# Mixer 0's recurrence: eight chunks formed at once, one product and one copy per chunk in the chain

## The chip, the cores and the metric

The kernel runs on 1 core of one Trainium2 chip. A core has five engines with their own instruction streams: TensorE (PE, matrix products into PSUM; its weight loads are shown as PEld), VectorE (DVE), ScalarE (ACT), GpSimd (POOL) and SyncE (SP, which issues DMAs). PSUM has eight banks; one bank holds 128 x 512 float32. The metric is the device time of one execution in microseconds (us); lower is better.

## The reference

A causal trunk of two layers over 1024 tokens of width 1024. All that the change touches is mixer A of layer 0, the RWKV-7 recurrence, 8 heads of 64:

```
xs = rms_norm(x) @ w_in ... shifted, split into r, k, v and low-rank w, a, g
decay w = exp(-exp(w_log));  kk = k*k_k / |k*k_k|;  k = k*(1 + (a-1)*k_a)
per head, per token t (S is 64 x 64, starts at 0):
    sa = S @ (-kk_t)
    S  = S * w_t + sa (x) (kk_t*a_t) + v_t (x) k_t
    y_t = S @ r_t
y: group norm per head, + bonus, * gate g; concatenated with mixer B (gated conv of width 3) @ w_out, added to h
```

After that mixer come a squared-ReLU MLP, a per-layer embedding, and layer 1 (a diagonal state-space mixer, its MLP and embedding) and a last RMSNorm. Those parts are as they were.

## The kernel before, in words

**Layout.** Activations are kept feature-major: 128 features on the partitions, 512 tokens (half the sequence) on the free axis. The sequence is done as two halves, A and B. A pair of heads fills 128 partitions, so a half has four pairs, and mixer 0 has eight (half, pair) units, numbered 0 to 7. Within a unit the 512 tokens are 8 chunks of 64.

**The large products.** Each float32 matrix product with a weight is three fp32r products (high and low halves of both operands, `mm3`, L157 to L159). One "unit" of filler work is one such triple: a tile `ps_z` of the input projection has 8 of them (`zmm`), a tile of the output projection (`ps_wo`, jobs named W) has one per input block. Weights come by DMA on SP's queue (`wload`, L142), are rounded by ACT (L145), and POOL forms the low half (L146).

**The recurrence of one (half, pair).** Four generators, each a list of steps divided by `yield`:

- `rwkv_f`: decay, its running product `L`, `eL`, the norm of kk (tiles `ps_w`, `ps_a`, `ps_ss`, `ps_rn`).
- `rwkv_a`: the scaled operands `RA` (r and -kk times the decay since the chunk's start) and `KB` (k and kk*a divided by it); the masked score matrices `SC` of every chunk (`ps_sc`); the bonus (`ps_bo`); then `inverse`: the inverse of a unit triangular 64 x 64 matrix per chunk and head, by doubling in 32 x 32 blocks (`ps_ix`, `ps_it`, `ps_fx`, `ps_ft`), each product followed by a VectorE operation that the next product needs. Its result is `Rf`.
- `rwkv_c`: first `V`, `K`, `B` with tokens on the partitions (`by_token`: four transposes and four ACT copies each, L687 and L691). Then for each chunk, in turn, with the state `S`: `ps_c` = scores x V + RA x S, an ACT copy to `rhs` (L725); `ps_sa` = Rf x rhs, an ACT copy to `SA` (L735); `ps_s` = K x V + B x SA, and VectorE makes the new state from it (`Sn`, L747) with the old state scaled by ACT (`SD`, L730); `ps_y` gives the output of the chunk, copied by VectorE to `Y` (L748). Three steps a chunk, 24 in all, each one waiting on a copy out of PSUM that the step before it made possible.
- `rwkv_g`: group norm of `Y`, transposes back (`ps_yt`, L779), gain and bias, the gate product (`ps_gt`, L788), and the split for the output projection (`yah`, `yal`).

**What sets the order.** TensorE's order is written by hand (`manual_schedule`); the other engines' orders are made by a scheduler at build time. `mixer0_run` goes through ten stages. In a stage up to four generators run side by side for different pairs (`crit`: for example c of pair 1, a of pair 2, g of pair 0, f of pair 3), one step of each at a time; after each step of theirs, units of the large products are put in (`MIX_JOBS` says which, `MIX_UNITS` how many in the stage; the stage has as many steps as its longest generator, `MIX_STEPS`). So TensorE's stream is: a burst of small products (one step of each generator), some units of three 512-column products as cover, the next burst, and so on. Jobs: z = the projections for r, k, v of a pair, C = the three projections of a conv group, W = a piece of the output projection, X = load and transpose x of half B, S = swap of the residual halves through DRAM, R = the sum of squares of half A's residual for the next norm (23 `yield`s, nearly none with a TensorE product), L = the low-rank projections.

**Norm of the input.** The 1/rms of a half (`rstd`) is formed inside the first `zmm` that ends: product `ps_ms`, square root on ACT, reciprocal on DVE, product `ps_rs` (L213 to L223), all at one place in TensorE's order.

**PSUM.** Three banks for the large products (`ps_z`, `ps_wo`, `ps_xt`), two with tag `a` (f and a), three with tag `b` (c and g).

Of the kernel before, what the change touches and what calls it, by code (L numbers as in the profile page):

```python
# [5 lines left out]
F32 = mybir.dt.float32  # L6
# [51 lines left out]
class Trunk:  # L58
# [16 lines left out]
    def setup2(self):  # L75
# [11 lines left out]
        mp = self.mp  # L87
        self.lwa = mp.tile([P, 512], F32, name="lwa")
# [400 lines left out]
    def zmm(self, st, col, out):  # L489
# [8 lines left out]
        if "rstd" not in st:  # L498
            st["rstd"] = list(self.rstd_steps(st["acc"], pool=self.pc, tag="a"))[1][0]
# [88 lines left out]
    def rwkv_f(self, st, p, cx):  # L588
# [38 lines left out]
        for _ in range(5):  # L627
            yield
# [6 lines left out]
    def rwkv_a(self, st, p, cx):  # L635
# [968 lines left out]
```

## Time and profile before

| | us |
|---|---|
| median of 3 runs | 2757.8 (2756.29 to 2758.71) |
| the profiled execution | 2759.97 |
| its span, first to last instruction | 2758.1 |
| end of mixer 0 (last `ps_wo` product) in that span | about 749 |
| TensorE busy over the span | 2608.0 |

A row of the timeline reads: start, duration, engine, line, operation, out<-in, count; the brackets give the idle time of the engine before it and what ended it. A float32 product of two operands that are not rounded shows two records per instruction, an fp32r product one. A product's duration is longer than the distance to the next one, since products overlap in the array; the price of a product in a stream is read from the starts. The view of stretches gives, for each stretch of time, the busy time of each engine with its count of instructions, the granted TensorE clock (PEclk, 1.00 is full speed) and the share of the DMA engines.

### The profile page before, as it was taken

Reading aid. Unit: us, or ns where it says so; the run is one execution under the profiler, and the core shown is the slowest. Engines: PE = TensorE matmul, PEld = TensorE weight load, DVE = VectorE, ACT = ScalarE, POOL = GpSimd, SP = SyncE. Lnnn points to the kernel's source line nnn. Section 1 sums busy time; section 2 is a strip of 40 time slices with the busy share of each in tenths; the row PEclk is TensorE's granted clock in tenths of the full one; section 3 lists DMA queues with packets and bytes.
Section 4 is the critical chain, followed back from the end, with each engine's and each line's share of the span. In section 5 each row is a group of like instructions: output and inputs, shape, how many; then the busy total and the mean of one; then the engine's idle time right before and its main releaser. Section 6 shows DMA issues by size and latency. Waiting matters only on the chain.

```text
span 2758.1 us, 47137 instructions
## 1 busy us (share of the span) xinstructions
PE 2608.0 (95%) x18029; PEld 2043.5 (74%) x18029; DVE 1933.9 (70%) x3103; ACT 1089.9 (40%) x2145; POOL 1195.4 (43%) x1771
## 2 busy tenths in 40 slices
PE   7999899999898899999999997999999999999998
PEld 5776676666576677777788776788788888888786
DVE  5565666665599899899778648622577777777854
ACT  4334444443432344454554535412433333333432
POOL 4443334532443577777764406411343443343410
PEclk9999999999999899999999999999999999999999
DMA  4222211411211233333121324311111111111121
GB/s 108 58 69 87 91 56 45 142 44 41 73 47 43 64 93 95 92 96 96 61 65 45 92 64 145 104 46 46 35 54 53 47 54 50 50 54 47 49 77 61
DMA packets 273437, 189.08 MB, mean 69 GB/s; under 512 B 36110, under 2 KB 255484, under 8 KB 273212
## 3 DMA queue, kind: packets, MB, share of 16 engines
q1 hardware_dynamic: 249232, 158.26, 19.4%
q10 hardware_dynamic: 21084, 19.17, 2.7%
q0 software_dynamic: 2896, 8.65, 0.9%
q8 instruction: 142, 2.33, 0.3%
q14 instruction: 83, 0.68, 0.1%
HBM read 156.92 MB, written 29.10 MB: 67 GB/s over the span
## 4 chain that ended last, share of the span: by engine, by line
PE 66%; DVE 15%; POOL 7%; issue 6%; ACT 3%; DMA 2%; SPq 0%; ACTq 0%; POOLq 0%; DVEq 0%
PE ps_dnx L352 9%; PE ps_up L159 6%; PE ps_up L157 6%; PE ps_up L158 6%; PE ps_dny L352 5%; PE ps_z L157 3%; PE ps_z L158 2%; PE ps_z L159 2%; PE ps_gl L157 2%; PE ps_gl L159 2%; PE ps_gl L158 2%; DVE ha L355 2%; PE ps_g L157 2%; PE ps_g L159 2%; PE ps_g L158 2%
## 5 line engine op out<-in xcount | busy, mean ns | idle before, releaser
L158 PE MATMUL ps_up<-prl,uwh 128*128 128x512 f32 x1024 | 403.9, 394 | 2.5 <-DVE prl L175 2.5
L159 PE MATMUL ps_up<-prh,uwl 128*128 128x512 f32 x1024 | 406.2, 397 | 0.0
L157 PE MATMUL ps_up<-prh,uwh 128*128 128x512 f32 x1024 | 405.2, 396 | 0.7 <-ACT prh L174 0.7
L258 POOL TENSOR_TENSOR uwl<-uraw,uwh 128x512 fp32r<-128x512 f32 x136 | 187.7, 1380 | 170.3 <-ACT uwh L255 169.4
L158 PEld LDWEIGHTS ps_up<-prl,uwh 128*128 128x128 f32 x1024 | 193.8, 189 | 49.3 <-DVE prl L175 4.1
L157 PEld LDWEIGHTS ps_up<-prh,uwh 128*128 128x128 f32 x1024 | 194.1, 190 | 46.4 <-ACT prh L174 1.2
L159 PEld LDWEIGHTS ps_up<-prh,uwl 128*128 128x128 f32 x1024 | 193.3, 189 | 44.6
L352 PE MATMUL ps_dnx<-hidh,whi 128*128 128x512 f32 x480 | 197.7, 412 | 29.7 <-DVE ha L355 29.6
L146 POOL TENSOR_TENSOR wlo<-wraw,whi 128x1024 fp32r<-128x1024 f32 x66 | 159.7, 2421 | 138.2 <-ACT whi L145 137.2
L271 POOL TENSOR_TENSOR draw<-draw 128x128 f32<-128x128 f32 x120 | 59.8, 499 | 339.2 <-DMA draw<-in_l_ffn_down_dram 274.9
L355 DVE TENSOR_TENSOR h<-h,ps_dnx 128x512 f32<-128x512 f32 x240 | 163.8, 683 | 57.8 <-PE ps_dnx L352 56.4
L196 POOL TENSOR_TENSOR acc<-acc,sq 128x512 f32<-128x512 f32 x70 | 105.6, 1517 | 220.4 <-ACT sq L195 219.6
L352 PE MATMUL ps_dnx<-hidl,whi 128*128 128x512 f32 x480 | 189.0, 394 | 3.7 <-DVE hidl L317 3.7
L352 PE MATMUL ps_dnx<-hidh,wlo 128*128 128x512 f32 x480 | 189.2, 394 | 2.4 <-DVE wlo L281 2.4
L157 PE MATMUL ps_z<-prh,whi 128*128 128x512 f32 x416 | 190.6, 458 | 0.0
L255 ACT CAST uwh<-uraw 128x512 fp32r<-128x512 f32 x136 | 84.2, 619 | 243.4 <-PE ps_up L158 227.7
L355 DVE TENSOR_TENSOR ha<-ha,ps_dnx 128x512 f32<-128x512 f32 x240 | 163.4, 681 | 18.4 <-PE ps_dnx L352 18.2
L145 ACT CAST whi<-wraw 128x1024 fp32r<-128x1024 f32 x104 | 108.8, 1047 | 166.5 <-PE ps_z L158 72.0
L159 PE MATMUL ps_z<-prh,wlo 128*128 128x512 f32 x416 | 168.1, 404 | 1.6 <-POOL wlo L146 1.6
L158 PE MATMUL ps_z<-prl,whi 128*128 128x512 f32 x416 | 167.7, 403 | 0.6 <-DVE prl L478 0.6
L317 DVE TENSOR_TENSOR hidl<-r_up,hidh 128x512 fp32r<-128x512 f32 x188 | 151.9, 820 | 21.2 <-ACT r_up L313 16.4
L312 ACT ACTIVATE hidh<-r_up 128x512 fp32r<-128x512 f32 x98 | 61.9, 632 | 232.9 <-DVE r_up L309 226.3
(429 smaller groups left out, 6623.7 us busy)
## 6 DMA issues: line engine op xcount, KB each, us to landing
uraw<-in_l_ffn_up_dram SPq DMA_DIRECT2D x128, 256.0 KB
draw<-in_l_ffn_down_dram SPq DMA_DIRECT2D x120, 256.0 KB
wraw<-in_l_w_in_dram SPq DMA_DIRECT2D x52, 512.0 KB
s5w<-s5w SPq DMA_DIRECT2D x32, 384.0 KB
wraw<-in_l_w_out_dram SPq DMA_DIRECT2D x16, 512.0 KB
wraw<-in_l_ple_gate_dram SPq DMA_DIRECT2D x16, 512.0 KB
wraw<-in_l_glu_w_dram SPq DMA_DIRECT2D x16, 512.0 KB
toep<-kt ACTq DMA_DIRECT2D x32, 240.0 KB
```

The source lines that it names most:

```text
L145: nc.scalar.copy(hi[:, :n], raw[:, :n])
L146: self.lo_engine().tensor_sub(lo[:, :n], raw[:, :n], hi[:, :n].bitcast(F32))
L157: nc.tensor.matmul(ps, wh, xh, start=start, stop=False)
L158: nc.tensor.matmul(ps, wh, xl, start=False, stop=False)
L159: nc.tensor.matmul(ps, wl, xh, start=False, stop=stop)
L196: (eng or nc.vector).tensor_add(acc, acc, sq)
L255: A.copy(uw[m][0], raws["u"])
L258: nc.gpsimd.tensor_sub(uw[m][1], raws["u"], uw[m][0].bitcast(F32))
L312: A.activation(st[n][0], r, AF.Square)
L317: return lambda: eng.tensor_sub(st[nm][1], t, st[nm][0].bitcast(F32))
L352: nc.tensor.matmul(ps, w[:, a], v, start=id(ps) not in begun, stop=n == 2, skip_group_check=True)
L355: V.tensor_add(hv, hv, ps)
```

## The change

The recurrence is rewritten so that nothing but one product and one copy per chunk depends on the chunk before:

- For all 8 chunks at once, one bank each: `X` = scores x V (`ps_x`), `W` = Rf x At (`ps_wc`, where `At` is the -kk part of RA by token, a fourth `by_token`), `U` = Rf x X (`ps_u`), `T` = I + W x B (`ps_t`), `Yr` = RA + W x scores (`ps_yr`). X, W and U are copied out by ACT, T and Yr by VectorE additions (T with the new constant `eye`).
- `pG` holds K x V + B x U of all chunks in one bank of its own; in the chain, `ps_g` of chunk c gets T x S added, and one ACT copy scaled by the chunk's decay is the next state. After the last chunk `ps_y` is made for all chunks (three products a chunk) and copied by ACT once.
- `rwkv_a` has its VectorE work and scores in fewer, fuller steps; `inverse` begins right after the first scores. `rwkv_g` has the gate product one step after the transposes back.
- `MIX_STEPS` falls from 26/28/7/6/13 to 14/14/5/6/8; the jobs and units of the stages are dealt out anew (`W67a` from the start of its stage into a mix with the norm of half B, `C1` to `C7` later or earlier by a place, `R` behind `W45b` in the next stage, `W67b` into the last stage).
- `rstd` of each half is formed by a generator `scale` with a step between its products, filled with units.
- PSUM: tag `b` has two banks in place of three; the third is `g`.

```diff
-MIX_STEPS = [26, 28, 7, 6, 13]
-MIX_UNITS = [19, 52, 78, 51, 73, 47, 57, 42, 44, 38, 5]
-MIX_JOBS = ['z1 C0', 'C1 z2 C2 W45a', 'z3 X3', 'W67a M L z4 W01a', 'C4 z5', 'z6 W23a C5', 'z7 S W45b R', 'C6 W01b', 'C7 W67b', 'W2b W3b', '']
+MIX_STEPS = [14, 14, 5, 6, 8]
+MIX_UNITS = [19, 48, 64, 72, 72, 48, 40, 48, 40, 40, 24]
+MIX_JOBS = ['z1 C0', 'z2 C1 W45a', 'z3 C2 X3', 'N M L z4 W01a', 'z5 C4', 'z6 W23a', 'z7 C5 S', 'W45b R C6', 'W01b C7', 'W67b W2b W3b', '']
...
+        self.eye = mp.tile([P, 64], F32, name="eye")
+        nc.vector.tensor_add(self.eye, self.ident[:, 0:64], self.ident[:, 64:128])
...
-        if "rstd" not in st:
-            st["rstd"] = list(self.rstd_steps(st["acc"], pool=self.pc, tag="a"))[1][0]
...
+        def scores(m):
             for g in range(2):
                 ps = self.pc.tile([P, H], F32, tag="a", name="ps_sc")
                 for q in range(4):
                     for h in range(2):
                         hs = slice(64 * h, 64 * h + 64)
-                        nc.tensor.matmul(ps[hs, q * P:(q + 1) * P], KB[hs, m, 4 * g + q], RA[hs, 4 * g + q], start=True, stop=True)
+                        nc.tensor.matmul(ps[hs, q * P:(q + 1) * P].rearrange("p (a t) -> p a t", a=2), KB[hs, m, 4 * g + q],
+                                         RA[hs, :, 4 * g + q], start=True, stop=True)
                 nc.vector.tensor_mul(SC[m][:, 4 * g:4 * g + 4], ps.rearrange("p (c t) -> p c t", c=4),
                                      self.msc.rearrange("p (o t) -> p o t", o=1).broadcast_to([P, 4, P]))
-                yield
+        scores(1)
+        nc.vector.tensor_mul(KB[:, 0], v8(k2), v8(enL))
+        rk = cx["bo"] = self.rp.tile([P, H], F32, tag="rk", name="rk", bufs=3)
+        nc.vector.scalar_tensor_tensor(rk, r, self.c("l0_r_k", p), k2, ALU.mult, ALU.mult)
+        yield
+        inv = self.inverse(SC[1], cx)
+        next(inv)
+        scores(0)
+        yield
         ps = self.pc.tile([P, H], F32, tag="a", name="ps_bo")
         nc.tensor.matmul(ps, self.bd, rk, start=True, stop=True)
         nc.vector.tensor_mul(rk, ps, v)
-        yield from self.inverse(SC[1], cx)
-        yield
-
-    def by_token(self, src, tag):
-
-        nc = self.nc
-        ps = self.pc.tile([P, H], F32, tag="b", name="ps_" + tag)
+        yield from inv
...
-        def mm(ps, a, b, start, stop):
+        c8 = lambda n, k=1: self.rp.tile([P, 8, 64], F32, tag=n, name=n, bufs=k)
+
+        def bank(name, tag="b"):
+            return self.pc.tile([P, H], F32, tag=tag, name=name).rearrange("p (c f) -> p c f", f=64)
+
+        def mm(ps, c, a, b, start=True, stop=True):
             for s in hs:
-                nc.tensor.matmul(ps[s, 0:64], a[s], b[s], start=start, stop=stop, skip_group_check=True)
...
+                nc.tensor.matmul(ps[s, c], a[s], b[s], start=start, stop=stop, skip_group_check=True)
+
+        def each(ps, a, b):
+            for c in range(8):
+                mm(ps, c, a[:, c], b[:, c])
+
+        V, At, K, B = c8("Vt"), c8("At"), c8("Kt"), SB[:, :, 64:128]
+        flat = lambda t: t.rearrange("p c t -> p (c t)")
+        kb = cx["KB"]
+        self.by_token(flat(kb[:, 0]), K, "Kt")
+        self.by_token(flat(kb[:, 1]), B, "Bt")
+        yield
+        self.by_token(v, V, "Vt")
+        yield
+        self.by_token(flat(RA[:, 1]), At, "At")
+        yield
+        X = SK[:, :, 64:128]
+        px = bank("ps_x")
+        each(px, X, V)
+        nc.scalar.copy(X, px)
+        yield
+        pw = bank("ps_wc")
+        each(pw, Rf, At)
+        W = At
+        nc.scalar.copy(W, pw)
+        pu = bank("ps_u")
+        each(pu, Rf, X)
+        U = c8("U")
+        nc.scalar.copy(U, pu)
+        yield
+        pt = bank("ps_t")
+        each(pt, W, B)
+        T = Rf
+        nc.vector.tensor_add(T, pt, self.eye.rearrange("p (o t) -> p o t", o=1).broadcast_to([P, 8, 64]))
+        py = bank("ps_yr")
+        each(py, W, SB[:, :, 0:64])
+        Yr = RA[:, 0]
+        nc.vector.tensor_add(Yr, Yr, py)
+        yield
+
+        pG = bank("ps_g", "g")
+        for c in range(8):
+            mm(pG, c, K[:, c], V[:, c], c == 0, False)
+            mm(pG, c, B[:, c], U[:, c], False, False)
+        Sh = c8("Sh")
         S = self.state[p]
-        small = lambda n, k=2: self.rp.tile([P, 64], F32, tag=n, name=n, bufs=k)
+        last = cx["last"]
         for c in range(8):
...
+            if S is not None:
+                mm(pG, c, T[:, c], S, False, c == 7)
+            cx.setdefault("S", []).append(S)
+            if c < 7 or not last:
+                Sn = Sh[:, c + 1] if c < 7 else self.rp.tile([P, 64], F32, tag="S%d" % p, name="Sn", bufs=1)
+                nc.scalar.activation(Sn, pG[:, c], AF.Copy, scale=DC[:, c:c + 1])
+                S = Sn
+            if c < 7:
+                yield
         self.state[p] = S
-        cx["Y"] = Y
+        py = bank("ps_y")
+        for c in range(8):
+            mm(py, c, SK[:, c, 0:64], V[:, c], c == 0, False)
+            mm(py, c, SB[:, c, 0:64], U[:, c], False, False)
+            if cx["S"][c] is not None:
+                mm(py, c, Yr[:, c], cx["S"][c], False, c == 7)
+        Y = cx["Y"] = c8("Y")
+        nc.scalar.copy(Y, py)
+        yield
...
-            self.pc = E(tc.tile_pool(name="pcb", bufs=3, space=PSUM, reuse_waits="tile"))
+            pcb = E(tc.tile_pool(name="pcb", bufs=2, space=PSUM, reuse_waits="tile"))
             pca = E(tc.tile_pool(name="pca", bufs=2, space=PSUM, reuse_waits="tile"))
-            self.pc = TwoPools(a=pca, b=self.pc)
+            pcg = E(tc.tile_pool(name="pcg", bufs=1, space=PSUM, reuse_waits="tile"))
+            self.pc = TwoPools(a=pca, b=pcb, g=pcg)
             self.ep = E(tc.tile_pool(name="m0e", bufs=2, reuse_waits="tile"))
...
+        def scale(st):
+
+            yield
+            r = self.rstd_steps(st["acc"], pool=self.pc, tag="a")
+            next(r)
+            yield
+            st["rstd"] = next(r)[0]
+            yield
+
...
```

Three places in TensorE's order. In the rows, `ps_z` and `ps_wo` triples are filler units, a row is one or more instructions in turn, and the names are those of the sections above.

First, inside the recurrence of one unit while the inverse of the next runs beside it (the fifth stage, units 3 and 4). Before:

```order
L702 MATMUL ps_c<-Sn,RA 64x64 x2
L702 MATMUL ps_s<-Vt,Kt 64x64 x2
L672 MATMUL ps_sc<-RA,KB 64x128 x8
L157 MATMUL ps_z<-prh,whi 128x512
L158 MATMUL ps_z<-prl,whi 128x512
L159 MATMUL ps_z<-prh,wlo 128x512
L702 MATMUL ps_sa<-rhs,Rf 64x64 x2
L702 MATMUL ps_y<-Vt,SC 64x64 x2
L702 MATMUL ps_y<-Sn,RA 64x64 x2
L672 MATMUL ps_sc<-RA,KB 64x128 x8
```

With the change, one step of the chain:

```order
L160 MATMUL ps_z<-prl,whi 128x512
L161 MATMUL ps_z<-prh,wlo 128x512
L707 MATMUL ps_g<-Sh,Rf 64x64 x2
L842 MATMUL ps_ix<-T_5002,SC 32x32 x32
L159 MATMUL ps_z<-prh,whi 128x512
L160 MATMUL ps_z<-prl,whi 128x512
L161 MATMUL ps_z<-prh,wlo 128x512
```

A step of the chain is now two instructions (one per head) in place of three steps of up to six; three or four units of filler stand between such steps in this stage, five in the fullest. Over mixer 0 the runs of products between filler units fall from 246 to 137, the 64x64 products rise from 1008 to 1392 instructions, the by-token transposes from 96 to 128; the other counts are equal.

Second, where the group norm's transposes back and the gate product stand. Before:

```order
L159 MATMUL ps_z<-prh,wlo 128x512
L779 MATMUL ps_yt<-ident,Y 128x128 x4
L788 MATMUL ps_gt<-sg,glu_367 128x512
L702 MATMUL ps_s<-SA,Bt 64x64 x2
L702 MATMUL ps_y<-SA,SC 64x64 x2
L157 MATMUL ps_z<-prh,whi 128x512
```

With the change:

```order
L161 MATMUL ps_z<-prh,wlo 128x512
L799 MATMUL ps_yt<-ident,Y 128x128 x4
L707 MATMUL ps_wc<-At,Rf 64x64 x16
L707 MATMUL ps_u<-SC,Rf 64x64 x16
L679 MATMUL ps_bo<-rk,cst 128x512
L842 MATMUL ps_ix<-Tm,SC 32x32 x32
L159 MATMUL ps_z<-prh,whi 128x512
```

`ps_gt` is now a burst later; `ps_yt`, `ps_wc` and `ps_u`, all of tag `b` with its two banks, follow each other.

Third, the last part of unit 6's recurrence beside unit 7's inverse (the stage `W45b R C6`). Before, the two had filler between all steps:

```order
L702 MATMUL ps_sa<-rhs,Rf 64x64 x2
L702 MATMUL ps_y<-Vt,SC 64x64 x2
L702 MATMUL ps_y<-Sn,RA 64x64 x2
L828 MATMUL ps_it<-X,R_8088 32x32 x32
L157 MATMUL ps_wo<-yah,whi 128x512
L158 MATMUL ps_wo<-yal,whi 128x512
L159 MATMUL ps_wo<-yah,wlo 128x512
```

With the change:

```order
L842 MATMUL ps_ix<-T_7621,SC 32x32 x32
L707 MATMUL ps_g<-Sh,Rf 64x64 x2
L849 MATMUL ps_it<-X,R_7623 32x32 x32
L707 MATMUL ps_g<-Sh,Rf 64x64 x2
L842 MATMUL ps_ix<-T_7759,SC 32x32 x32
L707 MATMUL ps_g<-Sh,Rf 64x64 x2
L849 MATMUL ps_it<-X,R_7761 32x32 x32
```

The units that this part of the stage was to have are `R`'s `yield`s, which hold no product; the 24 units of `C6` come after it in one piece.

More of the change, by code (lines that the diff above doesn't have):

```diff
@@ L626, in rwkv_f @@
         nc.scalar.copy(sq.rearrange("p (n i) -> p n i", i=64), rn.rearrange("p (n o) -> p n o", o=1).broadcast_to([P, 8, 64]))
-        for _ in range(5):
+        for _ in range(3):
             yield
@@ L678, in rwkv_a, with by_token @@
         nc.vector.tensor_mul(rk, ps, v)
-        yield from self.inverse(SC[1], cx)
-        yield
-    def by_token(self, src, tag):
+        yield from inv
+    def by_token(self, src, t, name):
         nc = self.nc
-        ps = self.pc.tile([P, H], F32, tag="b", name="ps_" + tag)
+        ps = self.pc.tile([P, H], F32, tag="b", name="ps_" + name)
         for q in range(4):
             nc.tensor.transpose(ps[:, q * P:(q + 1) * P], src[:, q * P:(q + 1) * P], self.ident)
-        t = self.rp.tile([P, 8, 64], F32, tag=tag, name=tag, bufs=1)
         for h in range(2):
@@ L691, in by_token @@
                 nc.scalar.copy(t[64 * h:64 * h + 64, c:8:2], ps[64 * c:64 * c + 64].rearrange("p (q f) -> p q f", f=P)[:, :, 64 * h:64 * h + 64])
-        return t
     def rwkv_c(self, p, cx):
@@ L704, in bank @@
-        def bank(name):
-            return self.pc.tile([P, H], F32, tag="b", name=name)
-        V = self.by_token(v, "Vt")
+                nc.tensor.matmul(ps[s, c], a[s], b[s], start=start, stop=stop, skip_group_check=True)
[6 more added lines that the diff above has]
+        self.by_token(flat(kb[:, 0]), K, "Kt")
@@ L715, in rwkv_c @@
+        yield
[4 more added lines that the diff above has]
+        Sh = c8("Sh")
         S = self.state[p]
-        small = lambda n, k=2: self.rp.tile([P, 64], F32, tag=n, name=n, bufs=k)
+        last = cx["last"]
         for c in range(8):
-            first = S is None
-            D_c = DC[:, c:c + 1]
-            pa = bank("ps_c")
-            mm(pa, SK[:, c, 64:128], V[:, c], True, first)
-            if not first:
-                mm(pa, RA[:, c, 64:128], S, False, True)
-            rhs = small("rhs")
-            nc.scalar.copy(rhs, pa[:, 0:64])
-            pS = bank("ps_s")
-            mm(pS, K[:, c], V[:, c], True, False)
-            if not first:
-                SD = small("SD")
-                nc.scalar.activation(SD, S, AF.Copy, scale=D_c)
-            yield
-            pb = bank("ps_sa")
-            mm(pb, Rf[:, c], rhs, True, True)
-            SA = small("SA")
-            nc.scalar.copy(SA, pb[:, 0:64])
-            py = bank("ps_y")
-            mm(py, SK[:, c, 0:64], V[:, c], True, False)
-            if not first:
-                mm(py, RA[:, c, 0:64], S, False, False)
-            yield
-            mm(pS, B[:, c], SA, False, True)
-            mm(py, SB[:, c, 0:64], SA, False, True)
-            Sn = self.rp.tile([P, 64], F32, tag="S%d" % p, name="Sn", bufs=1) if first else S
-            if first:
-                nc.vector.tensor_scalar_mul(Sn, pS[:, 0:64], D_c)
-            else:
-                nc.vector.scalar_tensor_tensor(Sn, pS[:, 0:64], D_c, SD, ALU.mult, ALU.add)
-            nc.vector.tensor_copy(Y[:, c], py[:, 0:64])
-            S = Sn
-            yield
@@ L774, in rwkv_g @@
         nc.vector.tensor_mul(Yv, Yv, bc(s2))
-        for _ in range(2):
-            yield
+        yield
         ps = self.pc.tile([P, H], F32, tag="b", name="ps_yt")
@@ L1387, in scale0 @@
             nc.gpsimd.dma_start(self.rscr, next(r)[0])
+        def scale(st):
[5 more added lines that the diff above has]
+            yield
         A, B = {}, {}
         ya, yb = {}, {}
-        cx = [{} for _ in range(8)]
+        cx = [{"last": n > 3} for n in range(8)]
         st = lambda n: A if n < 4 else B
@@ L1444, in mixer0_run @@
         self.setup2()
+        r = scale(A)
+        next(r)
+        for _ in range(4):
+            next(pre[2])
+        next(r)
+        for _ in range(4):
+            next(pre[2])
+        next(r)
         go([], pre[:3], 0)
```

29 lines of the change are left out of this document (9 added, 20 removed).

## The prediction

> **What bounds the kernel now.** I read the page first, for the engine that fills the span.
>
> ```profile
> PE 2608.0 (95%) x18029; PEld 2043.5 (74%) x18029; DVE 1933.9 (70%) x3103; ACT 1089.9 (40%) x2145; POOL 1195.4 (43%) x1771
> ```
>
> TensorE is busy 95% of the span, so a change is worth what it takes out of TensorE's own stream: product time, waits, and time at a lower clock. The change lies in mixer 0 alone, which ends near 749. So next the view of stretches, for the mixer and for pieces of it:
>
> ```profile
> 0.00:749.80 749.80, 690.16 (x9168) 505.06 (x9169) 449.46 (x743) 300.05 (x601) 301.90 (x309) 0.96 0.25 75
> 0.00:118.70 118.70, 99.89 (x989) 74.68 (x990) 69.05 (x95) 42.17 (x57) 54.77 (x71) 0.93 0.34 87
> 118.70:213.40 94.70, 92.48 (x1183) 69.49 (x1182) 58.06 (x87) 33.81 (x66) 42.54 (x39) 1.00 0.23 67
> ...
> 286.00:384.80 98.80, 88.45 (x1157) 65.39 (x1156) 62.78 (x100) 41.22 (x80) 38.34 (x38) 0.95 0.24 73
> ...
> 535.50:611.60 76.10, 68.06 (x1069) 48.78 (x1068) 49.75 (x81) 34.67 (x73) 33.38 (x34) 0.91 0.21 65
> ```
>
> After its length a row has the busy time of PE, PEld, DVE, ACT, POOL, each with its count, then the clock. The first row is the whole mixer, the others are pieces of it from one unit's `ps_Vt` to the next one's. TensorE idles 749.8 - 690.2 = 60 us. The clock, 0.96 over the mixer, takes 749.8 x 0.04 = 30 us more; it is lost in some pieces (0.91 to 0.95), and not at all in the second. The rest, about 660 us, is product time. Three pools of time then: 660, 60, 30. The waits by name:
>
> ```profile
> PE ps_gt L788 <- ACT gsq L783: 11.9, 7, 1.9
> PE ps_xt L461 <- DMA xraw<-in_x_dram: 10.7, 2, 6.0
> PE ps_rs L223 <- DVE rs L217: 7.6, 3, 4.1
> PE ps_wo L157 <- ACT ybh L796: 6.2, 1, 6.2
> PE ps_sa L702 <- ACT rhs L725: 3.3, 5, 0.7
> ...
> PE ps_wo L157 <- ACT yah L796: 2.1, 1, 2.1
> PE ps_yt L779 <- DVE Y L774: 2.0, 1, 2.0
> ```
>
> The recurrence that the change shortens hardly waits: its copies to `rhs` cost 3.3 us in five places. The filler already hides that chain. So the gain is not the shorter chain as such; it has to come from the three pools.
>
> **Product time: dearer products, fewer bursts.** One burst in the middle of filler:
>
> ```profile
> 398.25 0.39 PE L158 MATMUL ps_z<-prl,whi 128*128 128x512 f32 x1
> 398.47 0.40 PE L159 MATMUL ps_z<-prh,wlo 128*128 128x512 f32 x1
> 398.80 0.33 PE L702 MATMUL ps_c<-Vt,SC 64*64 64x64 f32 x4
> 398.96 0.28 PE L702 MATMUL ps_c<-Sn,RA 64*64 64x64 f32 x4
> 399.08 0.28 PE L702 MATMUL ps_s<-Vt,Kt 64*64 64x64 f32 x4
> 399.29 0.51 PE L157 MATMUL ps_z<-prh,whi 128*128 128x512 f32 x1
> 399.64 0.40 PE L158 MATMUL ps_z<-prl,whi 128*128 128x512 f32 x1
> ```
>
> By the starts, a pair of 64x64 products (both heads) takes 0.12 us in a run. The change adds 1392 - 1008 = 384 instructions, 192 pairs: 192 x 0.12 = +23 us. The fourth by-token turn adds 8 x 4 transposes:
>
> ```profile
> 677.56 0.60 PE L687 MATMUL ps_Kt<-ident,KB 128*128 128x128 f32 x4
> 677.91 0.47 PE L157 MATMUL ps_z<-prh,whi 128*128 128x512 f32 x1
> ```
>
> at 0.35 us for four, +3 us. Against this, a burst costs something by being a burst: filler to small product 0.33 where filler to filler is 0.23 (+0.10), the last group 0.21 to the filler where 0.12 would do (+0.09), the first filler product 0.35 (+0.12). That is 0.3 us, and there are 246 - 137 = 109 bursts fewer, -33 us. Product time: 23 + 3 - 33 = -7 us.
>
> **Waits.** The gate product first:
>
> ```profile
> 683.97 0.60 PE L779 MATMUL ps_yt<-ident,Y 128*128 128x128 f32 x4
> 686.22 1.12 PE L788 MATMUL ps_gt<-sg,glu 128*128 128x512 f32 x2 [1.65 <-ACT gsq L783]
> 684.66 1.50 ACT L783 COPY gsq<-ps_yt 64x256 f32<-64x256 f32 x4 [1.34 <-PE ps_yt L779]
> ```
>
> `ps_gt` waits for a bank that ACT is emptying. With the change it stands a burst later and doesn't. But tag `b` has two banks now, and `ps_yt`, `ps_wc`, `ps_u` follow each other: `ps_u` takes the bank of `ps_yt`, which is free at 686.16, 2.2 us after the first transpose. `ps_yt` (0.4) and `ps_wc` (8 pairs, 0.95) fill 1.35 of it, so 0.8 us of wait remains, in seven stages 6 us for 12. Behind `ps_u` stand `ps_bo` and the inverse's first product, which the DVE waits for: they come 0.8 us later and the following filler covers that. Gain 6 us.
>
> The norm's products: of 7.6 us, 3.5 (the second and third place) should vanish, with filler or other bursts between. At the first place a new wait takes over:
>
> ```profile
> 35.82 2.05 PE L223 MATMUL ps_rs<-ident,rs 128*128 128x128 f32 x8 [4.09 <-DVE rs L217]
> 42.16 0.63 ACT L517 ACTIVATE tw<-tw 64x512 f32<-64x512 f32 x1 [2.37 <-DVE tw L514]
> ```
>
> `ps_w`, which needs `tw`, could start 7 us after `ps_rs`. Eight units stood between; now one does, since seven have moved ahead of `ps_rs`, and they in turn need a third weight whose low half POOL forms in about 2.4 us (159.7 us in 66, below). I count nothing gained there. The end of the mixer had `ps_yt` and `yah` waiting 2.0 + 2.1 us with five units in the last stage; it has 24, -4 us. The chain's own waits on `rhs` (3.3 us) go, -3 us: a step of it has two to three times the cover. The 6.2 us on `ybh` stay: the last piece of conv group 3 still ends right ahead of W67a, and what is put between (`ps_Kt`, `ps_Bt`, `ps_ms`) is 1.9 us, while `ps_ms` itself needs the last squares of half B.
>
> ```profile
> L146 POOL TENSOR_TENSOR wlo<-wraw,whi 128x1024 fp32r<-128x1024 f32 x66 | 159.7, 2421 | 138.2 <-ACT whi L145 137.2 <-POOL Rf L852 0.5
> 657.00 0.75 PE L828 MATMUL ps_it<-X,R 32*32 32x32 f32 x64
> 657.80 0.42 DVE L830 TENSOR_TENSOR T<-T,ps_it 128x256 f32<-128x256 f32 x1 [0.38 <-PE ps_it L828]
> L730 ACT ACTIVATE SD<-Sn,DC 128x64 f32<-128x64 f32 x60 | 20.3, 345 | 83.5 <-DVE Sn L747 79.2 <-DVE Sn L745 4.0
> ```
>
> The stretch with no filler (stage `W45b R C6`): a hop of the inverse is product 0.75, then DVE 0.42, about 1.25 with the gaps; the next chain product and the change of shape use some 0.4 of the 0.5 between. The chain's scaled copy is 0.21 to 0.35 us (`rhs` and `SD`; no scaled copy out of PSUM of 64 columns stands here, I take 0.35) and fits in a hop. Eight hops at 0.3: +2.5 us. Taking the two heads' 64 columns of a score from two places may cost nothing or, as two products each, 2 x 0.12 against 0.24 now: nothing either way. ACT gains per unit four turn copies (quarters of `At`, 0.37 each below, +1.5), four copies of a whole bank (0.75 each, an estimate as twice such a quarter, +3) and eight scaled copies (8 x 0.35), and loses 16 copies of 0.21 and 7.5 scaled ones of 0.35 (6.0): +1.3 us a unit, on an engine busy for 300 of 750 us.
>
> ```profile
> L691 ACT COPY Kt<-ps_Kt 64x256 f32<-64x256 f32 x32 | 11.8, 368 | 1.6 <-PE ps_Kt L687 1.2
> ```
>
> The X, W, U copies have filler behind them; without that cover they would stop TensorE for some 0.75 us each, three a unit. DMAs: the same loads in another order on SP's queue, a weight at a time, a job ahead as before; `R`'s eight loads and its POOL-queue store come a stage later, still well ahead of the MLP that reads them.
>
> New waits from fuller steps are priced in rival (c); 6 us of its 60 go into the sum, its bounds being 0 and 60. Waits: -6 - 3.5 - 4 - 3 + 2.5 + 6 = -8 us.
>
> **Clock.** Where is it lost?
>
> ```profile
> 291.00:301.00 10.00, 6.46 (x16) 4.83 (x17) 7.85 (x10) 6.21 (x11) 2.87 (x2) 0.50 0.65 211
> 465.00:468.40 3.40, 1.75 (x14) 0.69 (x12) 1.94 (x2) 2.96 (x7) 1.51 (x2) 1.00 0.19 47
> 468.40:471.80 3.40, 3.40 (x18) 2.36 (x18) 2.24 (x5) 1.31 (x3) 0.00 (x0) 0.51 0.30 112
> ```
>
> After 3.4 us in which TensorE was busy for half, the clock is halved, for 3.4 to 10 us. The Trainium skill ("TensorE: Matmul & The Clock Gate", "What's actually happening") has the clock fall after an idle window of about 3.4 us. Here a window with a 1.65 us wait in it did it. By the page's rule only the two places with waits of over 3 us would cost clock, and both stay, so the clock term would be 0 and the time 2757.8 - 7 - 8 = 2743.
>
> By the rows, the places with 1.2 to 3 us of wait count, and most of those go (`ps_gt`, the later `ps_rs`, the end). What stays is the start (3.4 us of loss), the `ybh` place (5), and one or two more: 12 to 18 of 30. I take -12 us.
>
> **Sum.** -7 - 8 - 12 = -27 us. The profiled execution took 2759.97 with a span of 2758.1, 2.2 over the median; the terms are lengths inside the span and go over to the median: 2757.8 - 27 = 2731. What follows mixer 0 is unchanged and TensorE-bound, so the gain goes through.
>
> **Rivals.** (a) The gain is larger: if the filler covers all new waits (6 + 2.5 more) and the clock falls only at the start (another 13), 2731 - 8.5 - 13 = 2709. For it: bursts of small products alone kept the clock at 1.00 in the row 118.70. Against: the `ybh` place. (b) It cancels: two banks for three, and each wait that goes comes back elsewhere, so waits and clock are as before and the 7 us of products are all, 2757.8 - 7 = 2751. For it: `ps_u` stands just where `ps_gt` stood, and the chain was hidden anyway. (c) Slower, by DVE in the early steps of a stage. The work of `rwkv_a` up to the first inverse product is much of DVE's:
>
> ```profile
> L673 DVE TENSOR_TENSOR SC<-ps_sc,cst 128x512 f32<-128x512 f32 x32 | 21.8, 681 | 23.5 <-PE ps_sc L672 23.5
> L812 DVE TENSOR_TENSOR R<-SC,cst 32x256 f32<-32x256 f32 x32 | 21.1, 658 | 0.5
> ```
>
> These two are 4 x 0.68 and 4 x 0.66, 5.4 us a unit; the eleven other operations of it on 512 columns (counted in the code) at the same 0.68 are 7.5, nine of the group norm 6, and filler in the same time has 4 to 7. That is about 25 us, which had 15 of 28 steps (half of 64 to 81 us or more) and has 5 of 14 (20 to 30 us). If DVE gets only two thirds of those steps, its highest share in the pieces above (49.75 of 76.1), it needs 38 us where TensorE needs 25 or 30, and the pause halves the clock too: 7 to 10 us a stage, seven stages, 60 us: 2757.8 - 27 + 60 = 2791. It decides from 27 / 7, about 4 us a stage. Against it: much of that DVE work may run ahead in the late steps, which lose the state and `Y` operations. (d) That the chain isn't one product and one copy can't be: the order shows it.
>
> **How the numbers follow.** Forecast 2731: 0.50. Its own range is 2718 to 2745: its clock term between -6 and -18, its new waits between 0 and 14. (a) 2709: 0.18. (b) 2751: 0.18. (c) 2791: 0.14. This kernel's runs can't tell less than 0.2% (5.5 us) from no change. Faster is the forecast, (a) and half of (b), 0.77; within 0.2% the other half, 0.09; slower 0.14. For 8 in 10 the range reaches from 2703 to 2763: it holds (a) but for its far half, all of (b), and leaves (c) out.
>
> **What would show it.** Right: mixer 0 ends near 720; no wait at `ps_gt`, 0.5 to 1 us at `ps_u` in seven stages; the clock at 1.00 in most stretches; a state copy on ACT that nobody waits for. Wrong: TensorE waiting in each stage for SC, `R` or `Tm` from DVE (c); waits of 6 us or more between `ps_Kt` and `ps_t` for ACT's turn copies; a low clock all through the stretch without filler, which would say that small products don't hold it; or an unchanged end of mixer 0 with shorter waits, if the added products cost more than 0.12 a pair.

## The result, and the profile after

The changed kernel takes 2768.55 us (median of 5 runs, 2764.53 to 2769.96); the kernel before took 2756.29 in 5 runs beside it (2750.81 to 2758.71). The ratio is 1.0042, 95% interval 1.0028 to 1.0057: 12 us slower, where 27 us less were forecast. Yet mixer 0 itself became shorter. The profiled executions, cut at mixer 0's last `ps_wo` product and at the first `ps_pt` product (the end of layer 0's MLP):

| us | before | after | difference |
|---|---|---|---|
| mixer 0 | 750.2 | 736.0 | -14.2 |
| layer 0's MLP | 782.3 | 807.7 | +25.4 |
| the rest | 1225.6 | 1224.5 | -1.1 |
| span | 2758.1 | 2768.2 | +10.1 |

The MLP is code that the change doesn't touch. The view of stretches for the MLP, before:

```profile
750.00:1532.50 782.50, 735.25 (x3194) 578.12 (x3192) 688.61 (x1274) 364.15 (x867) 502.70 (x989) 0.98 0.26 72
```

and after, with mixer 0 above it:

```profile
0.00:736.00 736.00, 675.93 (x9970) 531.88 (x9970) 435.58 (x633) 295.55 (x530) 296.72 (x306) 0.96 0.26 76
736.00:1543.70 807.70, 742.96 (x3193) 585.69 (x3191) 698.75 (x1274) 367.14 (x869) 493.58 (x992) 0.97 0.26 71
```

In the MLP TensorE is busy for 743 us where it was 735, VectorE for 699 where it was 689; TensorE stands still for 17 us more (64.7 for 47.3), and 10 us more are lost to the clock (47.8 us at half clock for 27.3), together a little more than the 25. TensorE alone did not bound this part before either: it was busy for 94% of it, VectorE for 88%, and 29 of its 47 us of idle time were one kind of wait for VectorE. A row of waits reads: who waits, for whom, us in all, how many times, the longest. Who waits for whom there, before:

```profile
PE ps_dnx L352 <- DVE ha L355: 29.3, 30, 2.7
...
DVE hidl L317 <- ACT r_up L313: 13.3, 11, 2.4
```

and after:

```profile
PE ps_dnx L354 <- DVE ha L357: 46.1, 33, 3.8
...
DVE hidl L319 <- ACT r_up L315: 27.8, 18, 3.1
```

TensorE's down projection waits 17 us more for VectorE to empty its banks (`ha`, the residual), and VectorE waits 14.5 us more for `r_up` (the MLP's hidden values) from ACT. ACT and POOL also form, in this stage, tables for the state-space layer that follows: chains of small operations named `phase` and `pt`, alternating between ACT and POOL. Here is ACT's timeline around one cast of `whi`, before:

```profile
998.33 0.94 ACT L278 CAST whi<-draw 128x896 fp32r<-128x896 f32 x1 [4.15 <-POOL draw L274]
...
999.49 0.30 ACT L1098 ACTIVATE phase<-phase,wk 128x2 f32<-128x2 f32 x1 [0.22 <-issue]
...
1002.94 0.63 ACT L312 ACTIVATE hidh<-r_up 128x512 fp32r<-128x512 f32 x1 [2.96 <-DVE r_up L309]
```

and the same place after:

```profile
985.51 0.94 ACT L280 CAST whi<-draw 128x896 fp32r<-128x896 f32 x1
987.27 0.30 ACT L1119 ACTIVATE phase<-phase,wk 128x2 f32<-128x2 f32 x1 [0.82 <-POOL phase L1114]
...
989.30 0.30 ACT L1119 ACTIVATE phase<-phase,wk 128x4 f32<-128x4 f32 x1 [1.55 <-POOL phase L1121]
...
997.91 0.32 ACT L1119 ACTIVATE phase<-phase,wk 128x32 f32<-128x32 f32 x1 [2.63 <-POOL phase L1121]
...
998.58 0.63 ACT L314 ACTIVATE hidh<-r_up 128x512 fp32r<-128x512 f32 x1
```

Between the cast and the MLP's next `hidh` there was one step of the table's chain; now there are five (x2 to x32), each waiting for POOL. The work is the same; the scheduler has put it in another order on ACT and POOL. (Over the whole MLP the operations on `phase` and `pt` stand some 20 to 30 places earlier in the streams of ACT and POOL than before.) At the same place POOL's stream is denser, and something happens to VectorE:

```profile
983.57 5.51 DVE L319 TENSOR_TENSOR hidl<-r_up,hidh 128x512 fp32r<-128x512 f32 x2
...
983.99 1.30 POOL L319 TENSOR_TENSOR hidl<-r_up,hidh 128x512 fp32r<-128x512 f32 x1
...
985.24 0.69 POOL L1068 TENSOR_TENSOR CL<-LR,cx 128x288 f32<-128x288 f32 x1
...
985.87 1.29 POOL L260 TENSOR_TENSOR uwl<-uraw,uwh 128x512 fp32r<-128x512 f32 x1
...
992.43 0.80 PE L354 MATMUL ps_dnx<-hidh,whi 128*128 128x512 f32 x1 [3.78 <-DVE ha L357]
```

Two VectorE operations whose kind commonly takes 0.69 each (the median of the 94 in this MLP) take 5.51 (the first alone 4.85) beside a POOL that is busy for 5.58 of the 5.6 us from 983.5; `ha` follows late, and TensorE waits 3.78 us for it, the longest such wait of the MLP. The Trainium skill ("SBUF — State Buffer", "SBUF: two separate sides") says that a VectorE operation with two SBUF inputs and a GpSimd operation that reads SBUF lock each other out for a whole instruction. The trace agrees that VectorE stands still; here it stood for the length of several POOL instructions. All 94 such operations together took 84.1 us before and 87.5 after, while VectorE's wait for `r_up` grew by 14.5.

In mixer 0 the waits that the prediction named, after:

```profile
PE ps_wo L159 <- ACT ybh L817: 14.4, 4, 6.3
PE ps_xt L463 <- DMA xraw<-in_x_dram: 12.1, 3, 6.2
PE ps_w L599 <- ACT tw L517: 5.5, 1, 5.5
PE ps_u L707 <- ACT gsq L803: 5.1, 7, 1.5
PE ps_ms L215 <- POOL acc L198: 3.5, 1, 3.5
PE ps_wo L160 <- DVE ybl L818: 3.5, 3, 2.0
PE ps_wo L159 <- DVE h L584: 3.0, 2, 2.2
```

`ps_gt` (11.9 before) is gone, and `ps_u` waits 5.1 in its place, as forecast. But `ybh` and `ybl` (high and low half of a conv group's output) have grown from 6.2 + 2.7 to 14.4 + 3.5, in four places where a piece of the output projection stands right behind the conv group that it reads. In all, TensorE idles 60.1 us (59.6 before) and runs 58.0 us at half clock (64.9 before, a loss of 29.0 for 32.4). What is neither idle nor lost to the clock, 736.0 - 60.1 - 29.0 = 646.9, was 658.2: the product time fell by 11.3.

### The profile page after: what moved, and what is told of

Same layout as the page of the kernel before. It is cut to its first block, busy times and chain, and to the rows that moved or that the text cites. A ratio compares the mean times of both kernels' runs of the same rounds, so it can differ in the third digit from the quotient of the medians.

```text
span 2768.2 us, 48385 instructions
## 1 busy us (share of the span) xinstructions
PE 2601.9 (94%) x18829; PEld 2079.1 (75%) x18829; DVE 1928.5 (70%) x2992; ACT 1087.9 (39%) x2075; POOL 1178.5 (43%) x1771
## 3 DMA queue, kind: packets, MB, share of 16 engines
q1 hardware_dynamic: 249232, 158.26, 19.5%
## 4 chain that ended last, share of the span: by engine, by line
PE 66%; DVE 14%; POOL 8%; issue 5%; DMA 3%; ACT 3%; SPq 0%; ACTq 0%; POOLq 0%; DVEq 0%
PE ps_dnx L354 9%; PE ps_up L161 6%; PE ps_up L159 6%; PE ps_up L160 6%; PE ps_dny L354 4%; PE ps_z L159 3%; PE ps_z L160 3%; PE ps_z L161 3%; PE ps_gl L159 2%; PE ps_gl L161 2%; PE ps_gl L160 2%; DVE ha L357 2%; PE ps_dnz L354 2%; PE ps_g L159 2%; PE ps_g L160 2%
## 5 line engine op out<-in xcount | busy, mean ns | idle before, releaser
L319 DVE TENSOR_TENSOR hidl<-r_up,hidh 128x512 fp32r<-128x512 f32 x188 | 158.8, 856 | 37.3 <-ACT r_up L315 30.8
L159 PE MATMUL ps_z<-prh,whi 128*128 128x512 f32 x416 | 175.8, 423 | 0.1
```

The source lines that it names most:

```text
L159: nc.tensor.matmul(ps, wh, xh, start=start, stop=False)
L319: return lambda: eng.tensor_sub(st[nm][1], t, st[nm][0].bitcast(F32))
```

## The experiments

The first question is whether the order on ACT and POOL makes the MLP longer (theory ORDER), or the state in which mixer 0 leaves the engines (theory HANDOVER). The second is where the rest of mixer 0's forecast gain stayed. In the experiments up to e9, but for e2 and e3, the MLP's order on ACT and POOL is held to that of the kernel before, so that only mixer 0 differs. Inside mixer 0 the scheduler stayed free in all of them, so a part of what an edit brings there can be a new order of the other engines. The holding code is the same in all of them, the table a list of positions:

```diff
+    def pin(self, mark):
+        ins = list(self.nc.cur_bb.bb.instructions)[mark:]
+        for eng, order in FFN_ORDER.items():
+            mine = [i for i in ins if i.engine == eng and "Tile" not in type(i).__name__]
+            order = [int(x) for x in order.split()]
...
+            for a, b in zip(order, order[1:]):
+                self.tc.add_manual_dep(mine[b], mine[a].name, mybir.DependencyInfo(
+                    mybir.DependencyClass.NoSync, mybir.DependencyReason.DATA), reason="order")
...
                 self.mixer0(hp1, cp)
+            mark = len(nc.cur_bb.bb.instructions)
...
                         self.ffn(l, st["xn"], st["rstd"], done2, hook)
+                    if l == 0:
+                        self.pin(mark)
```

The results in one table: time (median), ratio to the kernel before run beside it, and the parts of the profiled execution, which is one execution and can stand some us from the median (7 in e9, 2750.3 for 2743.0).

| run | time, us | ratio (95%) | mixer 0 | MLP | rest |
|---|---|---|---|---|---|
| e1 | 2748.1 | 0.9974 (0.9956 to 0.9992) | 739.8 | 783.8 | 1226.8 |
| e2 | 2778.2 | 1.0082 (1.0056 to 1.0107) | 752.0 | 801.8 | 1228.1 |
| e3 | 2774.6 | 1.0060 (1.0038 to 1.0083) | 743.2 | 800.1 | 1227.9 |
| e4 | 2733.4 | 0.9920 (0.9896 to 0.9944) | 714.3 | 789.3 | 1226.2 |
| e5 | 2732.9 | 0.9920 (0.9898 to 0.9942) | 714.3 | 789.3 | 1224.7 |
| e6 | 2730.9 | 0.9912 (0.9887 to 0.9936) | 714.5 | 788.8 | 1224.8 |
| e7 | 2726.9 | 0.9893 (0.9873 to 0.9914) | 713.3 | 786.7 | 1226.4 |
| e8 | 2722.4 | 0.9875 (0.9850 to 0.9900) | 707.6 | 788.7 | 1227.1 |
| e9 | 2743.0 | 0.9948 (0.9928 to 0.9968) | 734.6 | 785.9 | 1227.8 |
| e10 | 2734.7 | 0.9919 (0.9894 to 0.9944) | 706.6 | 801.0 | 1228.0 |

### e1 to e3: whose loss it is

e1 is the changed kernel with the MLP's order of before.

> The changed kernel, with the instructions of ACT and POOL between mixer 0 and the end of layer 0's MLP held in the order that they had in the kernel before (ordering edges without a wait; mixer 0 and TensorE's own order as changed). Theory ORDER: the 25 us that the MLP of layer 0 lost (780.2 to 805.5 us from mixer 0's last ps_wo to 1530/1541) come from the order in which ACT and POOL run the s5 phase operations among the MLP's. Then the MLP takes about 780 again, mixer 0 ends at about 736 as in the changed kernel, and the time is 2768.5 - 25 = 2743 (2738 to 2750). Theory HANDOVER: the MLP is slower because of how mixer 0 leaves it (late weights, clock, a VectorE that is full whatever comes before): then 2768 as changed (2763 to 2772).

e2 is the kernel before with the MLP's order of the changed kernel.

> The reverse: the kernel before, mixer 0 untouched, with the order of the changed kernel on ACT and POOL in the MLP of layer 0. ORDER: 2757 + 20 to 25 = 2777 to 2782, mixer 0 ending at about 750 as before, TensorE waiting some 45 us for ha in the MLP where it waited 29. HANDOVER: 2757.

e3 is one number:

```diff
-MIX_STEPS = [26, 28, 7, 6, 13]
+MIX_STEPS = [26, 28, 7, 6, 12]
```

> The kernel before with one number of the first stage changed (the decay work of unit 1 starts one step earlier, 12 for 13), so that mixer 0 does the same work in nearly the same order, but the scheduler's order of ACT in the MLP comes out as that of the changed kernel and POOL's close to it (its phase operations 8 places earlier among the MLP's, the changed kernel's 14). ORDER: mixer 0 ends within 2 us of 750, the MLP takes 15 to 25 us more, 2770 to 2782. HANDOVER: 2757 +- 3.

All three came out as ORDER has it, and HANDOVER, as the cause of the 25 us, fails three times. Of the 25.4 us, e1 takes back 23.9 and e2 brings 19.5 without the new mixer. With the old order the changed kernel takes 2748.1, 0.26% less than before, and its MLP's waits are those of before:

```profile
PE ps_dnx L354 <- DVE ha L357: 28.0, 29, 2.7
...
PE ps_up L159 <- ACT prh L176: 5.6, 1, 5.6
...
DVE hidl L319 <- ACT r_up L315: 13.2, 11, 2.3
```

The middle row is new: in e1, and in e4 to e8, which also have the old order behind a changed mixer 0, the MLP begins with a wait of 5.6 us that neither the kernel before nor e9 has. So a few us do hang on how mixer 0 is left: e1's MLP is 1.5 us longer than that of the kernel before, those of e4 to e8 are 4 to 7 longer.

With the new order, behind the old mixer 0 (e2), the waits are those of after:

```profile
PE ps_dnx L352 <- DVE ha L355: 45.3, 34, 3.8
...
DVE hidl L317 <- ACT r_up L313: 20.7, 18, 2.6
```

and e3, in which the scheduler was free, has them too:

```profile
PE ps_dnx L352 <- DVE ha L355: 44.0, 31, 3.7
...
DVE hidl L317 <- ACT r_up L313: 22.8, 19, 2.6
```

So 18 to 24 us of the MLP hang on the order of ACT and POOL. In e2 and e3 the tables' chain stands 20 to 30 places earlier than before, as in the changed kernel, in e1 within three places of where it stood; but the whole order was held, so that the chain alone does it isn't shown. And one step of one generator in mixer 0's first stage is enough to turn it. (e3's mixer 0 also ended 7 us earlier than expected: with 59.3 us idle, as before, it ran 47.8 us at half clock for 64.9.) How much of the MLP's loss is the wait for `r_up` and how much the VectorE operations held up by POOL wasn't taken apart by a run, and why the scheduler turns the order isn't shown.

### e4: a conv group and the projection that reads it, apart

```diff
-MIX_UNITS = [19, 48, 64, 72, 72, 48, 40, 48, 40, 40, 24]
-MIX_JOBS = ['z1 C0', 'z2 C1 W45a', 'z3 C2 X3', 'N M L z4 W01a', 'z5 C4', 'z6 W23a', 'z7 C5 S', 'W45b R C6', 'W01b C7', 'W67b W2b W3b', '']
+MIX_UNITS = [19, 48, 48, 80, 72, 48, 40, 54, 40, 40, 24]
+MIX_JOBS = ['z1 C0', 'z2 C1', 'z3 W45a C2 X3', 'N M L z4 W01a', 'z5 C4', 'z6 W23a', 'C5 z7 S', 'W45b R C6', 'C7 W01b', 'W67b W2b W3b', '']
```

> As e1 (the MLP's order held to that of before), and in mixer 0 the pieces of the output projection no longer right behind the conv group that they read: W45a behind z3, C5 ahead of z7, C7 ahead of W01b. Theory NEAR (a wait counts where it stands, and goes when other filler stands in between): of the 14.4 + 3.5 us of waits on ybh and ybl, 13 to 15 go, and the clock falls in two or three places less (3.4 us of loss each): mixer 0 ends 13 to 22 us earlier than in e1, at 714 to 723, and the time is as much shorter, about 2726. Theory MOVES (a wait that goes comes back elsewhere, as seven of them did in the change): mixer 0 ends at 730 or later, the time is within 6 us of e1.

Mixer 0 ended 25.5 us earlier than in e1, a little more than NEAR had, and MOVES fails. The median fell by 14.7, to 2733.4 where NEAR had about 2726: the MLP behind is 5.5 us longer than e1's, and e1's profiled execution was 4 us above its median, e4's 2 below. No wait on `ybh` or `ybl` is left among its first rows:

```profile
PE ps_xt L463 <- DMA xraw<-in_x_dram: 12.4, 3, 5.4
PE ps_ms L215 <- POOL acc L198: 6.4, 1, 6.4
PE ps_u L707 <- ACT gsq L803: 6.0, 7, 2.5
PE ps_w L599 <- ACT tw L517: 5.5, 1, 5.5
```

One of the four did move: at the place of `N`, `ps_ms` now waits 6.4 where it waited 3.5 and `ybh` after it. Idle time fell from 61.5 to 48.9 us, the loss to the clock from 32.4 to 18.8, and product time stayed (645.9 and 646.6). The clock went along with the waits: 12.6 us of waiting less, and 13.6 less lost to the clock. One pair of profiles can't show that alone, since e3 lost 8.5 us less than the kernel before at the same idle time; all of them together do. The five with 59.3 to 61.5 us idle in mixer 0 (before, after, e1 to e3) lose 24 to 32 us to the clock there, the six with 41 to 50 (e4 to e8, e10) lose 14 to 19: on the mean 14.5 us less idle time and some 14 less loss.

### e5: more runs of small products

```diff
-                for c in list(crit):
+                for n, c in enumerate(list(crit), 1):
                     if next(c, self) is self:
                         crit.remove(c)
+                    while done < total * (step + n / 4) / nstep and unit():
+                        done += 1
                 step += 1
```

> e4 with the filler dealt out after each generator's part of a step in place of after all of them: the same products and the same number of filler units, but 226 runs of small products in place of 137. Theory BURST (a run of small products costs 0.3 us by being one, as the prediction had it): TensorE's busy time in mixer 0 rises by 89 x 0.3 = 27 us at full clock, less what shorter waits give back (up to 10 us): mixer 0 ends 15 to 27 us later than e4's 714.3, the time is 2733.4 + 15 to 27 = 2748 to 2760. Theory FREE (the saved 11 us of busy time came from something else): within 5 us of e4.

Neither theory: the time is that of e4, and TensorE's busy time rose, from e4's

```profile
0.00:714.30 714.30, 665.44 (x9970) 526.29 (x9970) 427.84 (x633) 291.70 (x524) 295.98 (x304) 0.97 0.26 78
```

to

```profile
0.00:714.30 714.30, 672.22 (x9970) 517.99 (x9970) 434.71 (x633) 290.89 (x524) 296.44 (x304) 0.98 0.27 78
```

by 6.8 us, or, with the clock taken out, 655.1 - 646.6 = 8.5: 0.1 us for each of the 89 added runs, not 0.3. e5 cuts a run where the shape of its products changes, and a change of shape has a price of its own (in e4's stream the starts are 0.15 apart from a 64x64 product to a 32x32 one, the median of 54 places, where a 64x64 product in a run takes 0.06). What a run costs beyond its products can be read from the starts around it, at full clock and where nothing waits. In the kernel before it is 0.34 us for 64x64 products alone (the median of 53 runs), 0.38 for 64x64 and 32x32 together (56), and nothing for transposes alone (32). In e5 32x32 products alone cost 0.24 (49). So cutting 64x64 from 32x32 products costs 0.2, and cutting transposes off costs nothing. The shorter waits (42.1 us idle for 48.9) and a little clock gave the 8.5 back. Fewer, fuller runs buy product time and pay for it in waits: here the two cancel.

### e6 to e8: the start, the stretch without filler, the bank of `ps_yt`

e6, on top of e4:

```diff
-        go([f(0, 0)], pre[3:], MIX_UNITS[0])
+        go([f(0, 2)], pre[3:], MIX_UNITS[0])
```

> e4 with the decay work of unit 0 two steps later in the stage that begins mixer 0, so that 8 units of filler stand between ps_rs and ps_w as before the change. The prediction counted nothing gained at the start; there TensorE waits 5.5 us for tw and the clock falls for 6.8 us behind it. If the wait is worth what it shows: -5 (the wait) - 3 (the clock) = -8 us against e4, mixer 0 ending at 706, 2725. Rival: the first stage ends by the chain through f and a of unit 0 (ps_sc and ps_bo wait for VectorE there), so that a later start of f only moves the wait: within 3 us of e4.

The 5.5 us at `ps_w` went. In their place stand 2.5 us at `ps_rn`, a later product of the same generator that now waits for ACT, and more at `ps_Vt`, 5.7 for 1.2.

TensorE runs 4 us earlier from 61 us on, and by the end of mixer 0 nothing of it is left (714.5). The interval of the time overlaps e4's. So the rival has it.

e7, on top of e4:

```diff
-MIX_JOBS = ['z1 C0', 'z2 C1', 'z3 W45a C2 X3', 'N M L z4 W01a', 'z5 C4', 'z6 W23a', 'C5 z7 S', 'W45b R C6', 'C7 W01b', 'W67b W2b W3b', '']
+MIX_JOBS = ['z1 C0', 'z2 C1', 'z3 W45a C2 X3', 'N M L z4 W01a', 'z5 C4', 'z6 W23a', 'C5 z7 S', 'W45b R', 'C7 W01b', 'W67b W2b W3b', '']
-                 "S": lambda q: [swap()], "R": lambda q: [scale0()],
+                 "S": lambda q: [swap()], "R": lambda q: [mix([scale0()], C(6), 1)],
-MIX_UNITS = [19, 48, 48, 80, 72, 48, 40, 54, 40, 40, 24]
+MIX_UNITS = [19, 48, 48, 80, 72, 48, 40, 54, 64, 40, 24]
```

> e4 with R's empty steps and the 24 units of C6 dealt out alternately, so that the stretch without filler (8 hops of unit 7's inverse with unit 6's chain) gets half a unit or more between steps. The prediction priced that stretch at +2.5 us. In e4 it has waits of some 0.26 us a hop, two of 0.7 and 0.9 put down to issue, and 10 us at half clock. If the stretch is what it costs: -3 (waits) - 5 (clock) = -8 us against e4, 2725, and the clock 1.00 through it. Rival: eight more runs of small products at 0.3 us take most of it: -2 or less.

In the changed kernel this stretch ran at a clock of 0.67:

```profile
619.00:640.00 21.00, 18.72 (x465) 16.79 (x466) 6.61 (x16) 4.49 (x12) 2.12 (x5) 0.67 0.08 26
```

With filler in it e7 has no half clock there (30.7 us in the whole mixer, 37.5 in e4, a loss of 3.4 less). Idle time and products took 2.4 of these back in the profile (mixer 0 ends 1.0 us earlier); the medians differ by 6.5, with overlapping intervals. So the stretch is worth 1 to 6 us: the profile sides with the rival (2 or less), the median is nearer to the 8 expected, and it isn't settled closer.

e8 is e4 with both and

```diff
-        ps = self.pc.tile([P, H], F32, tag="b", name="ps_yt")
+        ps = self.pc.tile([P, H], F32, tag="g", name="ps_yt")
```

> e4 with both of these and with ps_yt in the bank of ps_g, so that ps_u no longer waits for ACT to empty the bank of ps_yt (6.0 us in seven places in e4). If each is worth what its waits show: -8 - 8 - 6 = -22 us against e4, 2712, mixer 0 ending at about 692. If each wait comes back at the next thing that is late: -5 to -10.

2722.4 us: the best of the kernels here, 34 us less than before and 46 less than changed. Of the 22 us expected against e4 11 came in the median and 6.7 in mixer 0 of the profile, near the "-5 to -10" of waits that come back. `ps_u` no longer waits (idle time 41.3 us for 48.9), and what is left above all is the load of x (12.8 us in three places) and `ps_ms` (6.2).

### e9: one part of the change in the old recurrence

```diff
         nc.vector.tensor_add(y2, y2, bo)
+        yield
         ps = self.pc.tile([P, H], F32, tag="b", name="ps_gt")
```

> The kernel before with one part of the change alone: the gate product ps_gt a step after the transposes back (the MLP's order of ACT and POOL held to that of before, so that mixer 0 alone is compared). With three banks of tag b, nothing takes the bank of ps_yt in between. The prediction counted 11.9 us of waits in seven places for it. Theory WAITS GO: -11.9 and half of the clock places behind ps_gt (three of them, 1.7 to 3.4 us each), mixer 0 ending 12 to 20 us earlier than 750, 2737 to 2745. Theory MOVES: ps_s and ps_y behind it wait for the same copies or for VectorE's gsq, and the time is within 5 us of before.

Mixer 0 ended 15.6 us earlier and the time is 0.52% less: WAITS GO holds, though not all of them went for good. The wait on `gsq` is gone; 1.4 us at `ps_gt`, 1.7 at `ps_y` and 1.0 more at `ps_sa` came instead:

```profile
PE ps_gt L789 <- DVE Sn L745: 1.4, 1, 1.4
```

Idle time fell by 6.9 (to 52.7), the loss to the clock by 11.9 (to 20.5), and product time rose by 3.3. This one line, in the old recurrence, brings mixer 0 as much as the whole change did (15.6 and 14.2 us). How much of the 11.9 the waits brought isn't shown: e3 lost 8.5 less with the waits on `gsq` still there (12.5 us).

### e10: e8 with the scheduler free

e10 is e8 without the held order.

> e8 without the held order: the scheduler places ACT's and POOL's instructions in the MLP as in the changed kernel. ORDER: mixer 0 as in e8 (707.6, within 4 us), the MLP 15 to 25 us longer than e8's 788.7, so 2722 + 15 to 25 = 2737 to 2747. HANDOVER: 2722 +- 4, since the mixer that comes before is the same.

Mixer 0 is as in e8; the MLP takes 801.0 for 788.7, and its waits are again those of the changed kernel's order:

```profile
PE ps_dnx L354 <- DVE ha L357: 40.3, 30, 3.5
...
DVE hidl L319 <- ACT r_up L315: 24.3, 16, 3.0
```

ORDER holds behind a fourth mixer, though with 12 us, not 15 to 25; e8, with the old order, already had 6 us more than the MLP of before. Even so it is 0.8% faster than before.

## Why the prediction was wrong

- **"What follows mixer 0 is unchanged and TensorE-bound, so the gain goes through"** is the step that failed, and it alone turned the sign. TensorE's order in the MLP was unchanged; ACT's and POOL's were not, and TensorE waits there for VectorE (88% busy), which ACT and POOL feed. The MLP took 25 us more by the profile, and e1 to e3 show that the new order on ACT and POOL costs 18 to 24. "TensorE is busy 95% of the span" is an average over stages: in the 782 us of the MLP there were 47 us of idle time, 29 of them behind one kind of VectorE operation. Nor was mixer 0's own gain the one forecast: with the old order behind it the change brings 0.26%, some 7 us, not 27. The terms follow.
- **Product time, -7:** -11.3 measured. The sign and the weighing (192 dearer pairs against 109 fewer runs) fit: with the 0.34 to 0.38 us that most runs cost by the starts, the same sum gives -11 to -15. The 0.3 was read from one run, and it isn't a constant: a run of transposes costs nothing, and e5 has 0.1 where runs are cut at a change of shape.
- **Waits, -8:** +0.5 measured. `ps_gt` for `ps_u` came as worked out (11.9 for 5.1, forecast 6). "The 6.2 us on `ybh` stay" is the mis-sized term: 6.2 + 2.7 became 14.4 + 3.5, since the new deal of the jobs put two more projections right behind their conv groups (W45a and W45b wait 2.2 and 6.3 us), and W67b, which stood so before, waits 5.2 for 1.7. That stood in the job list, and the prediction priced one of the places only. With these apart (e4) waiting fell by 10.7 us against before, nearly the -8. In the rest of the sum, the waits on `rhs` are gone as forecast, the stretch without filler idles for 2.3 us in 21 (forecast 2.5), and new waits in the early steps of a stage come to 3.3 us where 6 were put (`ps_sc` 1.6, `ps_a` 2.2 for 1.2, `ps_bo` 1.2 for 0.5).
- **The norm's products, -3.5:** the two later `ps_rs` are gone, but `ps_ms`, which the term didn't price, waits 3.5 for the sum of squares. **The end, -4:** the waits on `Y` and `yah` went, and 2.2 us for `h` came. **The start:** `ps_w` waits 5.5 where `ps_rs` waited 4.1, nothing gained, as said.
- **Clock, -12:** -3.4 measured, with the waits as long as before. In e4, where they are shorter, it is -13.6 against before. One of the prediction's own signs of being wrong is there, too: the clock was 0.67 through the stretch without filler, some 7 us of loss that no term held. By the rule of the Trainium skill ("TensorE: Matmul & The Clock Gate", "What's actually happening") the term would have been 0. The record of the clock sides with the rows, which let shorter waits count (the windows are under the last heading), but not place by place: e1, with the changed kernel's TensorE order in mixer 0, has no gain of clock at all (64.9 us at half clock, as before), so that a clock term read from one profile is good to a few us only.
- **Rivals.** For mixer 0 alone (b) is nearest: -7 was its sum, -14.2 came, and waits did come back elsewhere. (c), VectorE in the early steps of a stage, did not happen: `ps_sc` waits 1.6 us for `KB` and `ps_bo` 1.2 for SC, once each, in the first stage. No rival had the MLP.

## What to carry to other kernels

Where a scheduler orders the other engines, a change in one stage can reorder a stage that it doesn't touch: before a gain is carried to the end, compare the order of every engine in the stages that follow, and ask which engine bounds each of them. When a change is measured, split the profile by stage first, and hold the order of the untouched stage to see the change alone. In this mixer a microsecond of waiting in TensorE's stream went with about one more lost to the clock, on the mean of the profiles and not at each place. What removed such waits was other work between the two ends (e4, e9), not a shorter chain that was already covered.

## What the runs showed of the hardware that was not expected

- A VectorE operation of 0.69 us (`hidl`, 128x512, two SBUF inputs) took 4.85 us beside POOL operations that followed each other without a gap. The longest of its kind took 4.6 to 4.9 us in all four kernels with the new order (changed, e2, e3, e10), and 1.8 to 2.9 in those with the order of before.
- The same stream of TensorE can lose a stretch of 6.8 us at half clock more or less: e1 and the changed kernel have the same TensorE order in mixer 0 and nearly the same idle time there (61.5 and 60.1 us), and 64.9 and 58.0 us at half clock. The Trainium skill ("TensorE: Matmul & The Clock Gate", "What's actually happening") has the window run freely; that would fit, and no run here tests it. A single profile tells mixer 0's end to some 4 us, and by e3 perhaps to 7.
- The clock's record goes in windows of 3.4 us. In mixer 0 of the twelve profiles, every window at full clock in which TensorE was busy for less than 1.45 us was followed by half clock (46 of 46). Of those with 1.45 to 1.9 us busy, half were (32 of 64), and of those with more, 13 of 2238. So with 1.5 to 2 us of idle time in one window it is open whether the clock falls, and what decides it there isn't shown.
- In the long stretch of small products TensorE stopped twice at `ps_ix` with nothing that the profile shows as its releaser: for 1.3 and 0.3 us in the changed kernel, 1.0 and 1.1 in e1, 0.7 and 2.1 in e5. What it waited for there is open.
